# Two experts of different groups in one strip of slots: a mixture-of-experts stage with four experts at a time

## The chip, the cores and the metric

The kernel runs on one core of a Trainium2 chip, in one launch. The metric is the device time in microseconds. A core has five engines that run their own instruction streams side by side and meet only at semaphores: TensorE (PE; the loading of its stationary operand is shown apart, as PEld), VectorE (DVE), ScalarE (ACT), GpSimd (POOL) and SyncE (SP). In this kernel SP does little but issue the loads of weights, in one fixed order.

## The reference

A decoder trunk of two layers over 256 tokens of width 1024, in float32. In each layer four attention mixers are summed into the residual, and then a mixture of experts is added:

```
lc  = x2 @ w_coarse + b_coarse              # 4 groups
grp = argmax(lc);  p_grp = softmax(lc)[grp]  # one group for a token
lf  = (x2 @ w_fine + b_fine)[grp]           # its 8 experts
two best of the eight, softmax over the two, times p_grp
x  <- x + gate2 * sum_e weight_e * (silu(a_e) * b_e) @ w2[e],   a_e, b_e = split(x2 @ w13[e])
```

There are 32 experts (4 groups of 8), w13 of 1024 x 512 and w2 of 256 x 1024 for each; so a layer reads 32 x 3.1 MB = 100.7 MB of expert weights, whatever the tokens choose. Each token goes to two experts of one and the same group. The change concerns only this part.

## The kernel before, in words

**The expert stage** (`experts`, from line 2015). The router (`route`) gives each token a rank among the tokens of its expert (`rk`) and a weight (`W`, split into a high and a low part). An expert has a strip of 64 slots (`CAP`), and two experts share the 128 rows of the array. For each of 16 pairs p the loop from line 2109 does this:

- `selection` makes 0/1 matrices from tokens to slots by comparing ranks with a row of slot numbers; `selection_t` transposes them, and `slot_weights` brings the tokens' weights to the slots. These serve two pairs (four strips) at once.
- `gather_bank`, in four banks for two pairs: the normalised tokens, as a high and a low part (`hh`, `hl`), are multiplied by the selection into 256 columns, scaled and shifted by the layer's modulation on the way out.
- `first`: the slots of the pair times w13, eight steps of 128 rows; expert e fills half e of the 128 output rows. `swiglu` and `hidden_t` make the hidden rows and transpose them.
- `second`: the hidden rows times w2, in two halves of 512 columns; `weighted` multiplies by slot weight and gate and splits into high and low.
- `scatter`, one turn later: the transposed selection brings the slots back to the tokens, into four accumulators that hold the residual stream and stay open for the whole stage.

`more_rounds` would repeat all this for experts with more than 64 tokens; its loop runs only if there are any.

**The loads.** `plan_all` fixes the order of all weight loads, and `advance` issues the next ones, on SP, as soon as a buffer is free: a ring of 8 buffers of 1 MB, and pages of 512 KB. A half of w13 (1 MB) takes a ring buffer or two pages, a half of w2 (512 KB) takes a page. `done` gives a buffer back after its last matmul. The order of the loads is the order of use, so a load that waits for its buffer holds up all behind it. After the last expert's weights come the first ones of the next layer (`in`, `ada`).

The order on TensorE around the stage is that of the program text: in turn p the first projection, the scatter of pair p-1, gather banks of the next two pairs, the hidden transposes, then the second projection:

```
            g = first(p)                                            # line 2119
            ...
                scatter(acc, ST[(p - 1) // 2][:, (p - 1) % 2], ys, False)
            if nxt:
                prep_g(q + 1, 3 * i)
            gT = hidden_t(g)
            if nxt and i == 0:
                prep_g(q + 1, 1)
                prep_g(q + 1, 2)
            elif nxt:
                prep_t(q + 1)
            ys = second(p, gT)                                      # line 2133
```

In layer 0 the small weights of layer 1's router (`load_weights`) and compression are fetched by ScalarE in turn 4. Names in the profile: `pg` pages, `ring` ring buffers, `at` working accumulators, `mm` the open ones, `gt` intermediate rows, `K` constants (the identity among them), `W` token weights.

Of the kernel before, what the change touches and what calls it, by code (L numbers as in the profile page):

```python
# [22 lines left out]
CAP = 64  # L23
# [235 lines left out]
def kernel(ctx, tc, x_in, c_in, w_ada, b_ada, norm_gain, w_in, qk_gain, cmp_pe, cmp_w1, cmp_w2,  # L259
# [1555 lines left out]

    rk = cst.tile([128, 2, NE], FT, name="rk")

    W = cst.tile([128, 2, 2, NE], FR, name="W")
    NRt = cst.tile([1, 17], I32, name="NRt")
# [3 lines left out]
    all1 = one_b.to_broadcast([128, 128])  # L1823

    def route(l, rs, lo):
# [29 lines left out]

        oh = T_("smb", [128, 2, 32], BF)
        V.tensor_tensor(oh, o12[:, :, 0], o12[:, :, 1], op=OP.add)
        p, tot = at([128, 2, 32]), at([128, 32])
        T.matmul(p[:, 0], tri, oh[:, 0], start=True, stop=True)
# [12 lines left out]
        V.tensor_scalar(rk, rk, -1.0, None, op0=OP.add)  # L1872
        cm = sm(16)
        V.tensor_reduce(cm[0:1], tot[0:1].rearrange("p (a b) -> p a b", b=2), axis=AX.X, op=OP.max)

        def further():

            nr = sm(17)
            V.tensor_scalar(nr[0:1, 0:16], cm[0:1], float(CAP), None, op0=OP.is_gt)
            for m in (2, 3):  # L1880
                V.scalar_tensor_tensor(nr[0:1, 0:16], cm[0:1], float(m * CAP), nr[0:1, 0:16], op0=OP.is_gt, op1=OP.add)
            V.tensor_reduce(nr[0:1, 16:17], nr[0:1, 0:16], axis=AX.X, op=OP.max)
            V.tensor_copy(NRt, nr[0:1])

        def weights():
# [4 lines left out]
            V.tensor_scalar(w3[:, :, 0], w3[:, :, 0], 0.5, None, op0=OP.mult)  # L1890
            V.tensor_tensor(w3[:, :, 1], w3[:, :, 0], e2, op=OP.mult)
            V.tensor_tensor(o12, o12, w3[:, :, :, None].to_broadcast([128, 2, 2, 32]), op=OP.mult)
            V.tensor_tensor(o12[:, :, 0], o12[:, :, 0], o12[:, :, 1], op=OP.add)
            split(W[:, :, 0], W[:, :, 1], o12[:, :, 0])

# [20 lines left out]
    def slot_weights(sel, ws, n):  # L1916
        p = at([128, n // 2, 2, 2])
# [4 lines left out]
        w = sm(n // 2)  # L1922
        for e in range(2):
            V.tensor_reduce(w[64 * e:64 * e + 64], p[64 * e:64 * e + 64, :, :, e], axis=AX.X, op=OP.add)
        return w

# [18 lines left out]

    def swiglu(p):
        th = T_("gt", [128, 256])
        A.activation(th, p[:, 0:256], AF.Tanh, scale=0.5)
        g = T_("gt", [128, 256])
        V.scalar_tensor_tensor(g, th, 1.0, p[:, 0:256], op0=OP.add, op1=OP.mult)  # L1950
        V.tensor_tensor(g, g, p[:, 256:512], op=OP.mult)
        return g

    def hidden_t(g):
        p = at([128, 2, 128])
        for k in range(2):
            T.transpose(p[:, k], g[:, 128 * k:128 * k + 128], ID)
        t = T_("gt", [128, 2, 128])
        A.activation(t, p, AF.Copy)
# [15 lines left out]
    def more_rounds(l, acc):  # L1975
        tot = nc.values_load(NRt[0:1, 16:17], min_val=0, max_val=3)
        with tc.If(tot > 0):
            with tc.For_i(0, NE // 2) as pi:
                rks = T_("sm", [128, 2, 2])
                V.tensor_copy(rks, rk[:, :, ds(2 * pi, 2)])  # L1980
                wsl = T_("sm", [128, 2, 2, 2], FR)
                V.tensor_copy(wsl, W[:, :, :, ds(2 * pi, 2)])
                rounds = nc.values_load(NRt[0:1, ds(pi, 1)], min_val=0, max_val=3)
                with tc.For_i(0, rounds):
                    V.tensor_scalar(rks, rks, float(-CAP), None, op0=OP.add)
                    sel, st = selection(rks, 2)
                    selection_t(sel, st, 2)
                    w = slot_weights(sel, wsl, 2)
# [3 lines left out]
                    p = at([128, 512])  # L1992
                    for k in range(KT):
                        for e in range(2):
                            t = T_("gt", [128, 512])
                            G.dma_start(t, w13[l, ds(2 * pi + e, 1), 128 * k:128 * k + 128, :]
                                              .rearrange("a p n -> p (a n)"))
                            T.matmul(p[64 * e:64 * e + 64], xg[k // 4][:, k % 4, 64 * e:64 * e + 64], t, start=k == 0,
                                     stop=k == KT - 1)
                    gT = hidden_t(swiglu(p))  # L2000
                    for n in range(2):
                        p = at([128, 512])
                        for k in range(2):
                            for e in range(2):
                                t = T_("gt", [128, 512])
                                G.dma_start(t, w2[l, ds(2 * pi + e, 1), 128 * k:128 * k + 128,
                                                        512 * n:512 * n + 512].rearrange("a p n -> p (a n)"))
                                T.matmul(p[64 * e:64 * e + 64], gT[:, k, 64 * e:64 * e + 64], t, start=k == 0,
                                         stop=k == 1)
                        y = weighted(p, w, MOD[l, "g2"][:, 512 * n:512 * n + 512])  # L2010
# [4 lines left out]
    def experts(l):  # L2015
# [40 lines left out]

        NP = NE // 2
        SEL, ST, SW, XG = {}, {}, {}, {}

# [4 lines left out]
        def prep_t(q):  # L2064
            selection_t(SEL[q], ST[q], 4)
            SW[q] = slot_weights(SEL[q], W[:, :, :, 4 * q:4 * q + 4], 4)

        def prep_g(q, b, eng=None):
            gather_bank(l, SEL[q], 4, b, XG[q], eng or (V if b % 2 else A))

        def first(p):
            q, i = divmod(p, 2)
            h = at([128, 512])
            for k in range(KT):
                for e in range(2):
                    w = piece(("w13", l, 2 * p + e, k // 4), (k % 4) * 512, 512)
                    c = 128 * i + 64 * e
                    T.matmul(h[64 * e:64 * e + 64], XG[q][k // 4][:, k % 4, c:c + 64], w,
                             start=k == 0, stop=k == KT - 1)
                if k % 4 == 3:  # L2080
                    for e in range(2):
                        done(("w13", l, 2 * p + e, k // 4))
            return swiglu(h)

        def second(p, gT):
            ys = []
            for n in range(2):
                y = at([128, 512])
                for k in range(2):
                    for e in range(2):  # L2090
                        w = tiles[("w2", l, 2 * p + e, k)]
                        T.matmul(y[64 * e:64 * e + 64], gT[:, k, 64 * e:64 * e + 64], w[:, 512 * n:512 * n + 512],
                                 start=k == 0, stop=k == 1)
                ys.append(weighted(y, SW[p // 2][:, p % 2:p % 2 + 1], MOD[l, "g2"][:, 512 * n:512 * n + 512]))
            for k in range(2):
                for e in range(2):
                    done(("w2", l, 2 * p + e, k))
            return ys
# [10 lines left out]
        for p in range(NP):  # L2109
            q, i = divmod(p, 2)  # L2110
            nxt = q + 1 < NP // 2
            if nxt and i == 0:
                prep_sel(q + 1)
            if l + 1 < DEPTH and p == 4:
                load_weights(l + 1)
                load_cw2(l + 1)
            if l + 1 < DEPTH and p == NP - 1:
                tables()
            g = first(p)
            if p == 0:  # L2120
                filler(2 - FILL)
                prep_t(0)
            else:
                scatter(acc, ST[(p - 1) // 2][:, (p - 1) % 2], ys, False)
# [83 lines left out]
```

## Time and profile before

| | |
|---|---|
| median of 3 runs | 1080.46 us (1079.86 to 1084.5) |
| profiled execution | 1081.84 us, its span 1080.1 us |
| TensorE busy | 1038.0 us, 96% of the span |
| VectorE, ScalarE busy | 597.3 us (55%), 446.0 us (41%) |
| moved from memory | 335.36 MB, 311 GB/s over the span |
| expert stages, first to last projection | 311 to 548 us (layer 0), 834 to 1071 us (layer 1) |

A busy TensorE is not a TensorE at its peak, since matmuls are pipelined; for its pace one reads the starts of its matmuls in the timeline. An f32 matmul has two records in the trace, and those of the two halves of the array stand side by side. The rate of the loads is read by stage, not over the span.

### The profile page before, as it was taken

The page shows a single profiled execution, that of the slowest core. Times are in us where ns is not written, and L with a number is a line of the kernel's source. Part 1 is how long each engine was busy: PE and PEld are TensorE (multiplying, and loading weights), DVE is VectorE, ACT ScalarE, POOL GpSimd, SP SyncE. Part 2 cuts the span into 40 slices and gives each one's busy share as a digit, 9 for nine tenths or more (in the row PEclk, how much of TensorE's full clock was granted, in tenths as well). Part 3 has the DMA queues.
Part 4 walks back from the last instruction along what each step waited for, and adds up shares of the span by engine and source line. Part 5 has one row for each costly group of instructions (what it writes and reads, how often), then busy time and mean ns, then how long its engine had stood idle before and what let it go on. Part 6 is the DMA issues. An engine that isn't in the chain of part 4 may idle for free. (4 is left out here: it accounts for less than half of the span.)

```text
span 1080.1 us, 15489 instructions
## 1 busy us (share of the span) xinstructions
PE 1038.0 (96%) x5615; PEld 654.6 (61%) x5616; DVE 597.3 (55%) x1316; ACT 446.0 (41%) x1089; POOL 136.4 (13%) x273
## 2 busy tenths in 40 slices
PE   5989999999999999999999989999999999999997
PEld 2557777787854455544446867778876554555542
DVE  1657678988653332333356885986876233333332
ACT  1554857754441222222146467667444222221211
POOL 0021444320010000000001342530201000000000
PEclk8999999999999999999999999999999999999999
DMA  9977765678899999999967784557779799999991
GB/s 337 412 240 285 270 203 198 219 274 312 311 346 362 410 343 410 411 412 412 413 237 239 267 335 162 197 195 255 290 262 373 265 410 352 411 412 410 412 393 40
DMA packets 151057, 337.50 MB, mean 312 GB/s; under 512 B 13197, under 2 KB 30909, under 8 KB 150973
## 3 DMA queue, kind: packets, MB, share of 16 engines
q1 hardware_dynamic: 144166, 334.66, 82.4%
q10 hardware_dynamic: 6678, 1.77, 0.7%
q8 instruction: 46, 0.75, 0.3%
q14 instruction: 39, 0.31, 0.1%
q0 software_dynamic: 128, 0.02, 0.0%
HBM read 335.36 MB, written 1.05 MB: 311 GB/s over the span
## 5 line engine op out<-in xcount | busy, mean ns | idle before, releaser
L253 PE MATMUL mm<-pg 128*128 128x512 f32 (+4 forms) x1984 | 467.8, 387 | 9.4 <-DVE pg L253 6.0
L253 PEld LDWEIGHTS mm<-pg 128*128 128x128 f32 x1984 | 350.8, 188 | 122.6 <-issue 36.6
L253 PE MATMUL at<-ring,pg 128*64 128x512 f32 (+2 forms) x912 | 241.1, 560 | 2.4 <-POOL pg L253 2.4
L253 PE MATMUL at<-pg 128*128 128x256 f32 (+6 forms) x1192 | 226.6, 363 | 3.1 <-ACT pg L253 1.9
L253 DVE TENSOR_TENSOR pg<-ring,pg 128x512 fp32r<-128x512 f32 (+4 forms) x276 | 182.1, 696 | 65.1 <-ACT pg L253 63.2
L253 PEld LDWEIGHTS at<-pg 128*128 128x128 f32 (+3 forms) x1192 | 130.5, 167 | 71.1 <-issue 56.8
L253 ACT ACTIVATE pg<-ring 128x512 fp32r<-128x512 f32 (+4 forms) x276 | 148.5, 600 | 18.2 <-DMA wr<-in_w_fine_dram 5.0
L253 PEld LDWEIGHTS at<-ring,pg 128*64 128x64 f32 (+2 forms) x912 | 80.4, 135 | 100.4 <-issue 87.0
L253 PE MATMUL at<-pg,gt 128*64 128x512 f32 x512 | 116.9, 598 | 2.1 <-ACT gt L253 2.1
L253 ACT ACTIVATE gt<-at 128x256 f32<-128x256 f32 x64 | 24.6, 384 | 214.5 <-PE at L253 207.8
L253 DVE SCALAR_TENSOR_TENSOR gt<-gt,at 128x256 f32<-128x256 f32 x32 | 13.5, 421 | 148.4 <-ACT gt L253 148.4
L253 ACT ACTIVATE pg<-gt 128x512 fp32r<-128x512 f32 x64 | 40.3, 629 | 115.5 <-DVE gt L253 115.5
L253 DVE SCALAR_TENSOR_TENSOR gt<-at,sm,pg 128x512 f32<-128x512 f32 x64 | 47.9, 748 | 61.7 <-PE at L253 61.7
L253 ACT ACTIVATE pg<-pg,sm 128x128 f32<-128x128 f32 (+2 forms) x168 | 70.1, 458 | 16.1 <-DVE sm L253 11.4
L253 ACT ACTIVATE pg<-at 128x512 f32<-128x512 f32 (+5 forms) x106 | 50.0, 502 | 54.1 <-PE at L253 53.8
L253 PEld LDWEIGHTS at<-pg,gt 128*64 128x64 f32 x512 | 33.9, 136 | 60.0 <-issue 51.7
L253 DVE TENSOR_TENSOR pg<-gt,pg 128x512 fp32r<-128x512 f32 x64 | 44.3, 692 | 45.7 <-ACT pg L253 44.3
L253 DVE TENSOR_SCALAR pg<-at,A,mod 128x256 f32<-128x256 f32 x64 | 31.7, 539 | 60.1 <-PE at L253 60.1
L253 PE MATMUL at<-K,pg 128*128 128x128 f32 (+1 forms) x388 | 59.4, 282 | 4.1 <-DVE pg L253 2.3
L253 ACT ACTIVATE gt<-mm 128x512 f32<-128x512 f32 x44 | 25.8, 595 | 78.6 <-PE mm L253 77.3
L253 DVE SCALAR_TENSOR_TENSOR pg<-ring,cs,pg 128x1024 f32<-128x1024 f32 x44 | 58.1, 1320 | 0.1
L253 PEld LDWEIGHTS at<-K,pg 128*128 128x128 f32 (+1 forms) x388 | 46.3, 143 | 18.3 <-DVE pg L253 4.7
(162 smaller groups left out, 678.7 us busy)
## 6 DMA issues: line engine op xcount, KB each, us to landing
pg<-in_w_dram SPq DMA_DIRECT2D x196, 512.0 KB, 10.9
ring<-in_w_dram SPq DMA_DIRECT2D x94, 1024.0 KB, 11.9
ring<-in_w_ada_dram SPq DMA_DIRECT2D x45, 1024.0 KB, 8.0
ring<-in_w_in_dram SPq DMA_DIRECT2D x33, 1024.0 KB, 4.8
ring<-in_cmp_w_dram SPq DMA_DIRECT2D x8, 1024.0 KB, 6.5
ring<-in_w_branch_dram SPq DMA_DIRECT2D x8, 1024.0 KB, 4.9
ring<-in_w_out_dram SPq DMA_DIRECT2D x8, 1024.0 KB, 4.8
ring<-in_w_in_dram SPq DMA_DIRECT2D x8, 976.0 KB
```

Source lines behind the costliest of these rows:

```text
L253: return f(*args, **kw)
```

## The change

A strip of 64 slots now belongs to two experts of different groups: expert p + 8s and expert p + 16 + 8s (s is the strip, 0 or 1; the second term is `b`). Since a token's two experts are of one group, it stands in a strip at most once. A turn of the loop handles two strips and four experts, so there are 8 turns in a layer. Selection, gather, slot weights, weighting and scatter are done once for a strip. Both experts' first projections run over all 64 slots; a mask of the slots (`m`, a third row of `W`) keeps of each slot the half of its own expert: `first_half` copies the first expert's product times its mask, `swiglu` adds the second's times the other mask, and then writes the hidden rows twice, once under each mask. The second projection sums both experts into the same accumulator. The loads of a turn are 8 halves of w13 and then 8 halves of w2. The fetch of layer 1's small weights moves from turn 4 of 16 to turn 2 of 8.

```diff
+    def expert(p, b, s):
+        return p + 16 * b + 8 * s
...
-            for p in range(NE // 2):
-                for hf in range(2):
-                    for e in range(2):
-                        add(("w13", l, 2 * p + e, hf))
-                for k in range(2):
-                    for e in range(2):
-                        add(("w2", l, 2 * p + e, k))
+            for p in range(NE // 4):
+                for b in range(2):
+                    for hf in range(2):
+                        for s in range(2):
+                            add(("w13", l, expert(p, b, s), hf))
+                for b in range(2):
+                    for k in range(2):
+                        for s in range(2):
+                            add(("w2", l, expert(p, b, s), k))
...
-        V.tensor_tensor(oh, o12[:, :, 0], o12[:, :, 1], op=OP.add)
+        o4 = o12.rearrange("p t i (h s u) -> p t u s (i h)", h=2, s=2)
+        for t in range(2):
+            V.tensor_reduce(oh[:, t].rearrange("p (u s) -> p u s", s=2), o4[:, t], axis=AX.X, op=OP.max)
...
+    def first_half(p, m):
+        t = T_("gt", [128, 512])
+        A.activation(t, p, AF.Copy, scale=m)
+        return t
+
-    def swiglu(p):
+    def swiglu(p, t, m):
+        V.scalar_tensor_tensor(t, p, m[1], t, op0=OP.mult, op1=OP.add)
         th = T_("gt", [128, 256])
-        A.activation(th, p[:, 0:256], AF.Tanh, scale=0.5)
-        g = T_("gt", [128, 256])
-        V.scalar_tensor_tensor(g, th, 1.0, p[:, 0:256], op0=OP.add, op1=OP.mult)
-        V.tensor_tensor(g, g, p[:, 256:512], op=OP.mult)
+        A.activation(th, t[:, 0:256], AF.Tanh, scale=0.5)
+        V.scalar_tensor_tensor(th, th, 1.0, t[:, 0:256], op0=OP.add, op1=OP.mult)
+        g = T_("gt", [128, 2, 256])
+        for b in range(2):
+            V.scalar_tensor_tensor(g[:, b], th, m[b], t[:, 256:512], op0=OP.mult, op1=OP.mult)
...
         def second(p, gT):
-            ys = []
-            for n in range(2):
-                y = at([128, 512])
+            ys = [at([128, 512]) for _ in range(2)]
+            for b in range(2):
+                for n in range(2):
+                    for k in range(2):
+                        for e in range(2):
+                            w = tiles[("w2", l, expert(p, b, e), k)]
+                            T.matmul(ys[n][64 * e:64 * e + 64], gT[:, b, k, 64 * e:64 * e + 64],
+                                     w[:, 512 * n:512 * n + 512], start=b == 0 and k == 0, stop=b == 1 and k == 1)
+                    if b:
+                        ys[n] = weighted(ys[n], SW[p // 2][:, p % 2:p % 2 + 1], MOD[l, "g2"][:, 512 * n:512 * n + 512])
                 for k in range(2):
                     for e in range(2):
-                        ...
+                        done(("w2", l, expert(p, b, e), k))
...
-            g = first(p)
+            h = first(p, 0)
...
+            h = first_half(h, masks(p)[0])
+            g = swiglu(first(p, 1), h, masks(p))
```

On TensorE, in the steady part of layer 0's expert stage, a turn of the program before, with two experts, from the scatter to the beginning of the next first projection (`mm<-pg` scatter, `at<-pg 128x256` gather, `at<-K,gt` hidden transposes, `at<-pg,gt` second projection, `at<-ring,pg` first projection):

```order
L253 MATMUL mm<-pg 128x512 x8
L253 MATMUL at<-pg 128x256 x8
L253 MATMUL at<-K,gt 128x128 x2
L253 MATMUL at<-pg 128x256 x16
L253 MATMUL at<-pg,gt 64x512 x8
L253 MATMUL at<-ring,pg 64x512 x8
```

And the same place in the changed program, a turn with four experts (here the other kind of turn, with the slot transposes `at<-K,pg` and slot weights `at<-W,pg`):

```order
L253 MATMUL mm<-pg 128x512 x8
L253 MATMUL at<-pg 128x256 x8
L253 MATMUL at<-K,gt 128x128 x4
L253 MATMUL at<-K,pg 128x128 x4
L253 MATMUL at<-W,pg 128x6 x4
L253 MATMUL at<-pg,gt 64x512 x16
L253 MATMUL at<-ring,pg 64x512 x17
```

Scatter and gather stand there with the same counts for four experts as before for two; hidden transposes and projections have twice the count.

On SP, in the same stage, the loads of one turn before (four halves of w13, `128x4x512` in the ring or twice `128x2x512` in pages, then four halves of w2, `128x1024`), with the semaphores that each waits for (DMAHW0 to 7 are those of earlier loads, PE and DVE stand for a buffer's last user):

```order
L320 DMA ring<-in_w_dram 128x4x512 [waits DMAHW0_49]
L320 DMA ring<-in_w_dram 128x4x512 [waits DMAHW1_49]
L320 DMA pg<-in_w_dram 128x2x512 [waits DMAHW2_49,PE_49]
L320 DMA pg<-in_w_dram 128x2x512 [waits DMAHW3_49,PE_49]
L320 DMA ring<-in_w_dram 128x4x512 [waits DMAHW4_49,PE_49]
L320 DMA pg<-in_w_dram 128x1024 [waits DMAHW5_49]
L320 DMA pg<-in_w_dram 128x1024 [waits DMAHW6_49]
L320 DMA pg<-in_w_dram 128x1024 [waits DMAHW7_49,PE_49]
L320 DMA pg<-in_w_dram 128x1024 [waits DMAHW0_49,DVE_49,PE_49]
```

And in the changed program, the last two halves of w13 of a turn, and its eight halves of w2:

```order
L320 DMA ring<-in_w_dram 128x4x512 [waits DMAHW0_49,PE_49]
L320 DMA ring<-in_w_dram 128x4x512 [waits DMAHW1_49,PE_49]
L320 DMA pg<-in_w_dram 128x1024 [waits DMAHW2_49]
L320 DMA pg<-in_w_dram 128x1024 [waits DMAHW3_49]
L320 DMA pg<-in_w_dram 128x1024 [waits DMAHW4_49]
L320 DMA pg<-in_w_dram 128x1024 [waits DMAHW5_49]
L320 DMA pg<-in_w_dram 128x1024 [waits DMAHW6_49,PE_49]
L320 DMA pg<-in_w_dram 128x1024 [waits DMAHW7_49,DVE_49,PE_49]
L320 DMA pg<-in_w_dram 128x1024 [waits DMAHW0_49,DMASW0_49,PE_49]
L320 DMA pg<-in_w_dram 128x1024 [waits DMAHW1_49,DVE_49]
```

Eight loads of w2 now follow each other, of which the last four wait for a page that an engine still uses.

## Rows read from the trace of the kernel before

**Rows 1.** Windows: start:end, length, busy time by engine, clock, DMA share, GB/s.

```profile
311.20:387.20 76.00, 75.79 (x398) 37.79 (x400) 25.24 (x52) 18.48 (x37) 0.00 (x0) 1.00 0.96 359
387.20:529.70 142.50, 142.50 (x736) 69.91 (x733) 48.44 (x94) 29.93 (x59) 0.00 (x0) 1.00 1.04 408
...
834.30:918.30 84.00, 84.00 (x434) 41.08 (x435) 28.05 (x57) 19.41 (x39) 0.00 (x0) 1.00 0.91 345
...
1050.00:1053.00 3.00, 3.00 (x15) 1.64 (x12) 0.84 (x2) 0.38 (x1) 0.00 (x0) 1.00 0.65 265
```

**Rows 2.** The page: rate of the loads in 40 equal slices of the span.

```profile
GB/s 337 412 240 285 270 203 198 219 274 312 311 346 362 410 343 410 411 412 412 413 237 239 267 335 162 197 195 255 290 262 373 265 410 352 411 412 410 412 393 40
```

**Rows 3.** Timeline of TensorE, four experts in layer 0: start, length, operation, count.

```profile
438.62 2.11 PE L253 MATMUL mm<-pg 128*128 128x512 f32 x8
...
441.65 2.16 PE L253 MATMUL at<-pg 128*128 128x256 f32 x16
443.74 3.65 PE L253 MATMUL at<-pg,gt 128*64 128x512 f32 x16
447.22 3.60 PE L253 MATMUL at<-ring,pg 128*64 128x512 f32 x16
...
454.19 2.14 PE L253 MATMUL mm<-pg 128*128 128x512 f32 x8
456.16 1.10 PE L253 MATMUL at<-pg 128*128 128x256 f32 x8
457.10 0.38 PE L253 MATMUL at<-K,gt 128*128 128x128 f32 x2
457.32 0.60 PE L253 MATMUL at<-K,pg 128*128 128x128 f32 x4
...
458.19 3.65 PE L253 MATMUL at<-pg,gt 128*64 128x512 f32 x16
...
468.64 0.73 PE L253 MATMUL mm<-pg 128*128 128x512 f32 x2
```

**Rows 4.** Waits, 387 to 530 us: total us, times, longest (weight loads; SP's queue).

```profile
PEld at L253 <- DMA pg<-in_w_dram: 0.6, 2, 0.3
SPq L320 <- PE at L253: 32.6, 24, 4.0
```

**Rows 5.** Timeline of SP: the last issues of expert weights, layer 0, layer 1.

```profile
514.96 4.80 SPq L320 DMA_DIRECT2D pg<-in_w_dram  x4
...
1037.28 4.81 SPq L320 DMA_DIRECT2D pg<-in_w_dram  x4
```

**Rows 6.** Timeline of TensorE, the ends of the two expert stages.

```profile
544.87 3.65 PE L253 MATMUL at<-pg,gt 128*64 128x512 f32 x16 [0.53 <-ACT gt L253]
...
559.37 1.06 PE L253 MATMUL mm<-ring,cs 128*32 128x512 f32 x8
...
1064.68 2.11 PE L253 MATMUL mm<-pg 128*128 128x512 f32 x8
...
1067.55 3.65 PE L253 MATMUL at<-pg,gt 128*64 128x512 f32 x16 [0.53 <-ACT gt L253]
```

**Rows 7.** Groups by shape, 403 to 530 us: busy us, mean ns, idle before.

```profile
L253 DVE SCALAR_TENSOR_TENSOR gt<-at,sm,pg 128x512 f32<-128x512 f32 x16 | 12.0, 748 | 13.7 <-PE at L253 13.7
...
L253 ACT ACTIVATE gt<-at 128x256 f32<-128x256 f32 x17 | 6.5, 384 | 57.2 <-PE at L253 57.2
L253 DVE SCALAR_TENSOR_TENSOR gt<-gt,at 128x256 f32<-128x256 f32 x9 | 3.8, 422 | 40.2 <-ACT gt L253 40.2
...
L253 ACT ACTIVATE pg<-at 128x512 fp32r<-128x512 f32 x4 | 2.4, 597 | 0.0
```

**Rows 8.** Start of the program: timeline of TensorE; a window as in rows 1.

```profile
13.04 1.06 PE L253 MATMUL mm<-ring,cs 128*32 128x512 f32 x8 [0.72 <-DMA ring<-in_w_ada_dram]
...
18.18 1.93 PE L253 MATMUL mm<-ring,cs 128*32 128x512 f32 x8 [4.08 <-DMA ring<-in_w_ada_dram]
...
16.00:27.00 11.00, 8.46 (x38) 6.27 (x39) 3.32 (x11) 3.53 (x8) 0.00 (x0) 0.55 1.03 406
```

More of the change, by code (lines that the diff above doesn't have):

```diff
@@ L1823, with strips_of @@
     all1 = one_b.to_broadcast([128, 128])
+    def strips_of(v):
+        return v.rearrange("p t (h s u) -> p t h u s", h=2, s=2)
     def route(l, rs, lo):
@@ L1891, in weights @@
             V.tensor_tensor(w3[:, :, 1], w3[:, :, 0], e2, op=OP.mult)
+            for t in range(2):
+                V.tensor_tensor(W[:, t, 2].rearrange("p (u s) -> p u s", s=2), *[
+                    o12[:, t, i, 0:16].rearrange("p (s u) -> p u s", s=2) for i in range(2)], op=OP.add)
             V.tensor_tensor(o12, o12, w3[:, :, :, None].to_broadcast([128, 2, 2, 32]), op=OP.mult)
-            V.tensor_tensor(o12[:, :, 0], o12[:, :, 0], o12[:, :, 1], op=OP.add)
-            split(W[:, :, 0], W[:, :, 1], o12[:, :, 0])
+            ws = T_("smb", [128, 2, 16])
+            for t in range(2):
+                V.tensor_reduce(ws[:, t].rearrange("p (u s) -> p u s", s=2), o4[:, t], axis=AX.X, op=OP.add)
+            split(W[:, :, 0], W[:, :, 1], ws)
         return further, weights
@@ L1921, in slot_weights @@
                          ws[:, t, :, 2 * i:2 * i + 2], start=t == 0, stop=t == 1)
-        w = sm(n // 2)
+        w, m = sm(n // 2), sm(n)
+        m = m.rearrange("p (b i) -> p b i", b=2)
         for e in range(2):
-            V.tensor_reduce(w[64 * e:64 * e + 64], p[64 * e:64 * e + 64, :, :, e], axis=AX.X, op=OP.add)
-        return w
+            r = slice(64 * e, 64 * e + 64)
+            V.tensor_reduce(w[r], p[r, :, 0:2, e], axis=AX.X, op=OP.add)
+            V.tensor_copy(m[r, 0], p[r, :, 2, e])
+        V.tensor_scalar(m[:, 1], m[:, 0], -1.0, 1.0, op0=OP.mult, op1=OP.add)
+        return w, m
     def gather_bank(l, sel, n, q, xg, eng):
@@ L1991, in more_rounds @@
                         gather_bank(l, sel, 2, q, xg, V)
[L1992 to L1999, printed above, removed]
@@ L2000, in more_rounds @@
-                    gT = hidden_t(swiglu(p))
+                    ms, t1 = [m[:, b] for b in range(2)], None
+                    for b in range(2):
+                        p = at([128, 512])
+                        for k in range(KT):
+                            for e in range(2):
+                                t = T_("gt", [128, 512])
+                                G.dma_start(t, w13[l, ds(pi + (16 * b + 8 * e), 1), 128 * k:128 * k + 128, :]
+                                                  .rearrange("a p n -> p (a n)"))
+                                T.matmul(p[64 * e:64 * e + 64], xg[k // 4][:, k % 4, 64 * e:64 * e + 64], t, start=k == 0,
+                                         stop=k == KT - 1)
+                        if b == 0:
+                            t1 = first_half(p, ms[0])
@@ L2001, in more_rounds @@
+                    gT = hidden_t(swiglu(p, t1, ms))
                     for n in range(2):
                         p = at([128, 512])
[L2003 to L2009, printed above, removed]
+                        for b in range(2):
+                            for k in range(2):
+                                for e in range(2):
+                                    t = T_("gt", [128, 512])
+                                    G.dma_start(t, w2[l, ds(pi + (16 * b + 8 * e), 1), 128 * k:128 * k + 128,
+                                                      512 * n:512 * n + 512].rearrange("a p n -> p (a n)"))
+                                    T.matmul(p[64 * e:64 * e + 64], gT[:, b, k, 64 * e:64 * e + 64], t,
+                                             start=b == 0 and k == 0, stop=b == 1 and k == 1)
@@ L2055, in experts @@
         seeds(1)
[L2057 to L2058 removed]
+        NP = NE // 4
+        SEL, ST, SW, SM, XG = {}, {}, {}, {}, {}
         def prep_sel(q):
@@ L2065, in prep_t, with first @@
             selection_t(SEL[q], ST[q], 4)
-            SW[q] = slot_weights(SEL[q], W[:, :, :, 4 * q:4 * q + 4], 4)
+            SW[q], SM[q] = slot_weights(SEL[q], W[:, :, :, 4 * q:4 * q + 4], 4)
         def prep_g(q, b, eng=None):
             gather_bank(l, SEL[q], 4, b, XG[q], eng or (V if b % 2 else A))
-        def first(p):
+        def first(p, b):
             q, i = divmod(p, 2)
@@ L2075, in first @@
                 for e in range(2):
-                    w = piece(("w13", l, 2 * p + e, k // 4), (k % 4) * 512, 512)
+                    key = "w13", l, expert(p, b, e), k // 4
                     c = 128 * i + 64 * e
-                    T.matmul(h[64 * e:64 * e + 64], XG[q][k // 4][:, k % 4, c:c + 64], w,
+                    T.matmul(h[64 * e:64 * e + 64], XG[q][k // 4][:, k % 4, c:c + 64], piece(key, (k % 4) * 512, 512),
                              start=k == 0, stop=k == KT - 1)
@@ L2081, in first, with masks @@
                     for e in range(2):
-                        done(("w13", l, 2 * p + e, k // 4))
-            return swiglu(h)
+                        done(("w13", l, expert(p, b, e), k // 4))
+            return h
+        def masks(p):
+            return [SM[p // 2][:, b, p % 2:p % 2 + 1] for b in range(2)]
         def second(p, gT):
-            ys = []
-            for n in range(2):
-                y = at([128, 512])
+            ys = [at([128, 512]) for _ in range(2)]
+            for b in range(2):
+                for n in range(2):
+                    for k in range(2):
+                        for e in range(2):
+                            w = tiles[("w2", l, expert(p, b, e), k)]
[3 more added lines that the diff above has]
+                        ys[n] = weighted(ys[n], SW[p // 2][:, p % 2:p % 2 + 1], MOD[l, "g2"][:, 512 * n:512 * n + 512])
                 for k in range(2):
                     for e in range(2):
[L2091 to L2097, printed above, removed]
+                        done(("w2", l, expert(p, b, e), k))
             return ys
@@ L2113, in experts @@
                 prep_sel(q + 1)
-            if l + 1 < DEPTH and p == 4:
+            if l + 1 < DEPTH and p == 2:
                 load_weights(l + 1)
@@ L2122, in experts @@
                 prep_t(0)
-            else:
+            h = first_half(h, masks(p)[0])
+            g = swiglu(first(p, 1), h, masks(p))
+            if p:
                 scatter(acc, ST[(p - 1) // 2][:, (p - 1) % 2], ys, False)
```

37 lines of the change are left out of this document (18 added, 19 removed).

## The prediction

> **What bounds the kernel now.** I began with the windows of the expert stages [rows 1]: TensorE is busy for all 142.5 of 142.5 us, which would suggest that any work taken from it shortens the program. The page's line of load rates warns against that [rows 2]: in slices 16 to 20 and 33 to 38, the later part of the two layers' expert stages, the loads run at 410 to 413 GB/s (one at 352), and no slice of the whole program shows more than 413. So two things are near their limit at once, and the question is which is ahead of the other, and by how much.
>
> The timeline of TensorE gives its pace [rows 3]. Two turns of the loop handle four experts: from the scatter at 438.62 to the scatter at 468.64, 30.02 us. The pace of the loads is 408 GB/s from 387 to 530 us [rows 1] and 411 at its steadiest [rows 2]. Four experts have eight loads of 1.05 MB and eight of 0.52 MB, 12.58 MB, which is 30.6 us at 411 GB/s. The loads are thus the slower of the two already, by 0.6 us in 30, and TensorE doesn't feel it because it lives on a stock: in the second half of layer 0 the weight loads into the array wait 0.6 us in all for an expert's load [rows 4]. At the end of a layer the stock can be read off. The last expert load of layer 1 is in the last issue group, 1037.28 plus 4.81, so issued by 1042.1 [rows 5]; the window from 1050 to 1053 moves at 265 instead of 411 GB/s [rows 1], so the stream ends at 1050 + 3 x 265/411 = 1051.9. The last second projection, which uses that load, starts only at 1067.55 [rows 6]. In layer 0 the last group is issued by 514.96 + 4.80 = 519.8 [rows 5]; with the lag of layer 1 (9.8 us) it lands at 529.6, and its projection starts at 544.87 [rows 6]. The stock at the end is 15.6 us in layer 1 and 15.3 us in layer 0.
>
> **The change part by part.** *What TensorE loses.* For four experts there is one scatter instead of two (454.19 to 456.16: 1.97 us), two gather banks instead of four (441.65 to 443.74: 2.09 us), and half of the slot transposes and slot weights (457.32 to 458.19: 0.87, half is 0.44) [rows 3]. First and second projections and the transposes of the hidden rows keep their count. 30.02 - 4.50 = 25.5 us, 36.0 us in a layer of eight such steps, 72 us in the program, if nothing else limited it.
>
> *What the loads allow.* No byte is saved: 12.58 MB for four experts, as before. Once TensorE has used up its stock of 15 us it waits, so most of the 36 us cannot be had. The end of a layer is then counted from the landing of its last load. The last eight loads are now the second-projection weights, 4.19 MB or 10.2 us of the stream; so the last first-projection load lands 10.2 us before the end of it. Behind that one come half of a first projection (a whole one takes 6.97, 447.22 to 454.19 [rows 3]: 3.5), and the way from the end of it to the second projection, 2.87 (1064.68 to 1067.55 [rows 6]) plus what the way gains: on VectorE a product over 512 columns at 0.75 and one more over 256 at 0.42 [rows 7], and four transposes and a 512-wide copy where two and 256 stood, some 0.3; 4.3 together. The second projection starts 10.2 - 7.8 = 2.4 us before the stream ends, runs twice 3.48 us, and ends 4.6 us after it. Before, it ended 15.6 + 3.5 = 19.1 us after it in layer 1 and 18.8 us in layer 0. That gives 14.5 and 14.2 us. It is the stock, given back; this is the firm part of the sum, 28.7 us.
>
> *What the stream itself gains.* It was held up by full buffers early in each expert stage: 359 GB/s over 76 us in layer 0, 345 over 84 us in layer 1 [rows 1]. Against 411 that is 9.6 and 13.5 us, the most that earlier freed buffers can return. They come free 4.5 us earlier at each step, the first ones not at all earlier, and in layer 0 the router and compression weights for layer 1 still go out in the middle of the stage. The other end is nothing. I take 5 us in each layer, near the middle and nearer the low end in layer 1, where the first window is the emptiest.
>
> *What is added, and its cover.* Masking the first expert's half is one ScalarE copy of 128x512 (597 ns), and the merge one VectorE operation like the 748 ns one [rows 7]; both engines are busy for less than half of the time here (48 and 30 of 142.5 us [rows 1]), and weighting and splits, halved in count, pay for it. The merge waits for the second of the two first projections; behind it on VectorE stand that step's gather evacuation, weighting and splits, all of which come later on TensorE too, so nobody waits for them sooner. In a full step the scatter and a gather bank (454.19 to 457.10: 2.91 [rows 3]) stand between the last first-projection matmul and the hidden transposes and cover the chain of 0.75 + 0.38 + three times 0.42 = 2.39 [rows 7], with its hand-overs just so; where that cover is gone, in the last two steps of a layer, the 1.2 us more is in the 4.3 above. The router is changed by a few operations on 16 instead of 32 columns, some more reduces of about 0.2 us, on a path of some 10 us: between -0.5 and +1 us in each layer; I take 0.
>
> *What the next layer meets.* Its first loads follow on the same stream: two of 1.05 MB and four of 1.05 MB land 5.1 and 15.3 us after the last expert load. TensorE used the four at 559.37 [rows 6], 11.0 us after the end of the last second projection at 548.35; now that is 4.6 + 11.0 = 15.6 us after the stream's end. They are just in time; layer 0's gain survives, with a microsecond or two at risk.
>
> *The sum.* The profiled execution took 1081.84 us, its span 1080.1; the median of the three runs is 1080.46. 14.2 + 14.5 + 5 + 5 = 38.7: a profiled time of 1043, and 1041.8 for the median. With the two unknown stream terms at their upper ends it is 28.7 + 23.1 = 51.8, or 1028.7; at nothing, 1051.8.
>
> The Trainium skill, DMA: Bandwidth & Descriptors, Specifications, gives 435 GB/s as the fabric's ceiling and about 358 GB/s as a core's share of HBM. The trace decides against the second: 411 GB/s stood for over 120 us. By the first, as an estimate, the long stretches of some 140 us would end 8 us earlier each, and the time would be about 1025; no slice of the page shows a rate above 413, so it stays out of the sum.
>
> **The rivals.**
> *TensorE sets the pace after all.* Then all 72 us but the longer chains are saved, about 1014 us. For it: TensorE has no idle time in 142.5 us [rows 1]. Against it: 100.7 MB in eight steps of 25.5 us would need 493 GB/s. 3%.
>
> *The loads set it already, nothing is gained.* 1080 us. For it: 30.6 against 30.0 us. Against it: were it so, the last load would be used when it lands, not 15 us later. It could still come true if a stage needed that stock for an irregularity that I don't see. 5%.
>
> *The eight pages stop the stream (slower).* A step's eight second-projection weights go only into pages, where four did before, and the last ones wait for pages that TensorE frees in the second projection of a step before; the first-projection loads of the next step stand behind them on the same queue. Already now the queue waits for TensorE 24 times, 4.0 us at the longest, 32.6 us in 142 [rows 4], hidden since up to eight loads are under way (the eight semaphores that its issues wait for in turn). If every one of the 16 steps lost a stretch t of the stream, the time is 1041.8 + 16 t: no gain at t = 2.4, slower by 0.5% from 2.8 us, 1106 at 4.0. Against it: a page is freed by the first half of the second projection now, and eight loads under way are 10 to 20 us of the stream. 5%.
>
> *The clock falls while TensorE waits (slower).* The start of the program shows it: after 4.08 us of waiting for a load eight matmuls took 1.93 us, where the same eight had taken 1.06, and the granted clock of 16 to 27 us was 0.55, mostly the lower level, 1.2 GHz [rows 8]. In the last two steps of each layer TensorE will wait some 1.7 us before a pair of first-projection loads (5.1 us of stream for 3.5 us of matmuls). If that dropped the clock for those four steps, each would take some 19 us longer: 1118 us. Against it: after a wait of 0.72 us the eight took the 1.06 us, and 1.7 lies nearer to that than to 4.08. 3%. The Trainium skill, TensorE: Matmul & The Clock Gate, HAM oscillation, warns of just this, a kernel whose short blocks of matmuls alternate with waits for loads and which starts each block cold; the row of 18.18 agrees with it, the wait here is shorter.
>
> That the change doesn't do what it says would be a strip of more than 64 tokens, which sends the program through the rounds loop; the reference's router, worked out on its own inputs, puts 52 and 53 tokens at most on a strip in the two layers. 1%.
>
> **How the numbers follow.** My forecast, the stream sets the end, has 83% and the range 1028 to 1056 by its two bounds and the risk at the next layer's start. The rivals have 3, 5, 5, 3 and 1%. For 8 in 10 I take 1028 to 1058. A measurement of this kernel can tell about 0.5% from no change, 5.4 us: faster has the forecast and the first rival and a little of the third, 87%; the same 5%; slower 8%.
>
> **What would show it.** Right: in both layers' last two steps first projections of 18 to 20 us, with TensorE idle for the expert loads; loads at 411 GB/s until a few microseconds before the layer's last projection; the steps before at about 25.5 us; the last second projection ending 4 to 6 us after the last load. Wrong: a step of 25.5 us up to the end (the first rival), loads below 400 GB/s in the second half of a stage with the queue waiting for TensorE (the pages), or a granted clock below 1 there.

## The result, and the profile after

The changed kernel takes 1065.91 us (median of 4 runs, 1063.65 to 1068.41) against 1080.64 (1079.86 to 1084.5) for the kernel before: a ratio of 0.986 [0.982, 0.989] (in brackets, here and below, the 95% interval). The sign was forecast, the size was not: 14.7 us are gained where 38.7 were forecast, and 1065.9 lies above the range of 1028 to 1058. The profiled execution took 1063.65 us, its span 1062.0.

In the page of the changed kernel, the line of load rates, 40 slices of the span, to be held against [rows 2]:

```profile
GB/s 354 398 261 268 282 205 199 191 286 336 300 339 375 394 346 392 395 394 395 394 394 277 259 327 162 201 193 244 288 339 242 350 364 394 395 395 395 391 391 207
```

No slice reaches 400. Where the kernel before stood at 410 to 413 for many slices, this one stands at 391 to 395. The second slice matters most: 398 instead of 412 [rows 2], although the two programs do the same there. Windows of the kernel before, from 27 to 54 us (columns as in [rows 1]: window, length, PE, PEld, DVE, ACT, POOL, clock, DMA share, GB/s):

```profile
27.00:54.00 27.00, 26.11 (x135) 16.08 (x133) 18.38 (x48) 15.03 (x35) 1.94 (x2) 1.00 1.03 411
```

The same window of the changed kernel, and three stretches of its expert stages (early part and later part of layer 0, later part of layer 1):

```profile
27.00:54.00 27.00, 25.67 (x132) 15.38 (x131) 17.80 (x47) 14.20 (x33) 1.94 (x2) 1.00 1.04 397
...
311.30:387.30 76.00, 74.65 (x377) 32.72 (x379) 18.45 (x43) 13.96 (x26) 0.00 (x0) 1.00 1.02 368
387.30:531.30 144.00, 128.35 (x580) 49.71 (x576) 29.21 (x58) 17.12 (x30) 0.00 (x0) 1.00 1.04 394
...
909.00:1045.00 136.00, 122.60 (x542) 47.93 (x538) 26.40 (x54) 15.87 (x28) 0.00 (x0) 0.99 1.04 395
```

So the loads are slower at 27 us already, long before an expert's weight is read, and they are slower while the DMA engines are busy all the time (share 1.04). In the later part TensorE is now busy for 128 of 144 us, where it was busy without a gap [rows 1]; the clock stays up.

What TensorE waits for is seen in the timeline of the end of layer 1 (start, length, operation, count, idle time before and what ended it), which answers to [rows 6]:

```profile
1011.70 2.11 PE L253 MATMUL mm<-pg 128*128 128x512 f32 x8
...
1035.66 1.07 PE L253 MATMUL at<-ring,pg 128*64 128x512 f32 x2 [0.39 <-DMA ring<-in_w_dram]
1038.37 3.65 PE L253 MATMUL at<-ring,pg 128*64 128x512 f32 x14 [1.63 <-DMA ring<-in_w_dram]
1041.94 2.11 PE L253 MATMUL mm<-pg 128*128 128x512 f32 x8
...
1045.88 7.09 PE L253 MATMUL at<-pg,gt 128*64 128x512 f32 x32 [0.69 <-ACT gt L253]
```

From scatter to scatter the last step takes 30.24 us, where 25.5 was worked out for TensorE's own pace, and the first projections in it wait for loads of w13 in the ring. And the waits from 387 to 530 us, which answer to [rows 4] (total us, times, longest):

```profile
PEld at L253 <- DMA ring<-in_w_dram: 23.8, 12, 2.8
...
SPq L320 <- PE at L253: 28.3, 17, 3.6
SPq L320 <- DMA ring<-in_w_dram: 22.0, 10, 2.6
```

The weight loads into the array wait 23.8 us for expert loads, where it was 0.6. SP's queue waits for TensorE no more than before (28.3 against 32.6), so the eight pages of the third rival do not hold the stream. What it waits for more than before are loads that are still under way: 22.0 us for those into the ring, where it was 9.6.

What differs at 27 us? Not the instructions, but the addresses. All buffers for loads follow the small tables in each partition of on-chip memory. The change made three of those shorter: `rk` from 256 to 128 bytes, `W` from 512 to 384, `NRt` from 68 to 36, 288 bytes together with its rounding. In the built programs the ring begins at byte 26880 of a partition before, which is 105 x 256, and at 26592 after, a multiple of 32 and not of 64; the buffers are multiples of 4096 long, so every one of them is shifted alike. The records of the loads' packets (a packet is one unbroken run of a load) show a difference of that kind: before, 97% of the 88,832 packets of 2048 bytes took 84 ns; after, 43% did, and most of the others 85 to 96.

### The profile page after: what moved, and what is told of

It reads as the page before. It is cut to its first block, busy times and chain, and to the rows that moved or that the text cites. A ratio compares the mean times of both kernels' runs of the same rounds, so it can differ in the third digit from the quotient of the medians.

```text
span 1062.0 us, 14314 instructions
## 1 busy us (share of the span) xinstructions
PE 991.4 (93%) x5167; PEld 598.9 (56%) x5168; DVE 538.2 (51%) x1220; ACT 407.5 (38%) x1001; POOL 136.5 (13%) x273
## 5 line engine op out<-in xcount | busy, mean ns | idle before, releaser
L253 PE MATMUL mm<-pg 128*128 128x512 f32 (+4 forms) x1856 | 435.0, 387 | 11.6 <-DVE pg L253 5.3
L253 PEld LDWEIGHTS mm<-pg 128*128 128x128 f32 x1856 | 330.3, 189 | 106.1 <-issue 22.8
L253 PE MATMUL at<-ring,pg 128*64 128x512 f32 (+3 forms) x888 | 241.9, 566 | 26.1 <-DMA ring<-in_w_dram 24.5
L253 PE MATMUL at<-pg 128*64 128x512 f32 (+6 forms) x960 | 193.8, 390 | 5.3 <-ACT pg L253 2.5
L253 PEld LDWEIGHTS at<-pg 128*64 128x64 f32 (+3 forms) x960 | 96.5, 160 | 62.6 <-issue 42.2
L253 DVE SCALAR_TENSOR_TENSOR gt<-at,sm,gt 128x512 f32<-128x512 f32 x16 | 12.0, 751 | 214.6 <-PE at L253 214.6
L253 DVE SCALAR_TENSOR_TENSOR gt<-at,sm,pg 128x512 f32<-128x512 f32 x32 | 23.9, 748 | 86.3 <-PE at L253 75.6
L253 ACT ACTIVATE pg<-gt 128x512 fp32r<-128x512 f32 x32 | 20.1, 630 | 114.0 <-DVE gt L253 114.0
L253 PEld LDWEIGHTS at<-K,pg 128*128 128x128 f32 (+1 forms) x356 | 43.7, 146 | 17.7 <-issue 4.4
L253 ACT ACTIVATE gt<-at,sm 128x512 f32<-128x512 f32 x16 | 11.0, 688 | 97.4 <-PE at L253 79.6
L253 POOL TENSOR_TENSOR pg<-pg,gt 128x512 f32<-128x512 f32 x16 | 29.6, 1874 | 107.3 <-DVE gt L253 107.3
## 6 DMA issues: line engine op xcount, KB each, us to landing
ring<-in_w_dram SPq DMA_DIRECT2D x91, 1024.0 KB, 13.1
```

Of the source, the lines that this page charges most:

```text
L253: return f(*args, **kw)
```

## The experiments

Theory A is that the address does it; B, that the order of the loads does (eight of w2 in a row); C, that the rate differs from run to run whatever the program.

**The addresses, within the kernels (e1 to e4, on one chip).** e1 is the changed kernel again; the others have one line more:

```diff
     sb = ctx.enter_context(tc.tile_pool(name="sb", bufs=1))
+    sb.tile([128, 8], FT, name="pad", tag="pad", bufs=1)     # e2, and e4 on the kernel before; 24 in e3
```

> The changed kernel as it is, a second time. Theory A (addresses): since the change made a few small tables shorter, all load buffers begin at 26592 bytes in a partition instead of 26880, which is a multiple of 32 but not of 64 bytes, and that slows every load; expected: saturated slices at 392 to 395 GB/s again, the same stretch at the start (27 to 54 us) at 397, 1064 to 1068 us. Theory B (the order of the loads and the eight w2 loads in a row slow the stream): the same numbers in the expert stages, but no reason for 397 at the start. Theory C (the rate of memory differs from run to run): anything between 392 and 412 GB/s, time between 1042 and 1068.

> The changed kernel with an unused 32 bytes ahead of the buffers, so that they begin at 26624, a multiple of 512; nothing else differs. A: 410 to 412 GB/s in the saturated slices and 411 at 27 to 54 us, and the time falls by about 20 us against e1, to 1042 to 1048. B: 392 to 395 GB/s in the expert stages and e1's time. C: the rate and the time of e1, since both run on one chip, or a difference without order.

> As e2 with 96 bytes: the buffers begin at 26688, a multiple of 64 but not of 128 or 256. If a multiple of 64 is what counts, e2's rate and time (410 GB/s, 1042 to 1048 us); if a multiple of 256 is, e1's (394 GB/s, 1066) or something between. B and C: e1's numbers.

> The kernel before with 32 unused bytes ahead of its buffers, so that they begin at 26912, not a multiple of 64. A: 392 to 397 GB/s where it had 410 to 412, the saturated steps of the loads then 31.9 us against TensorE's 30.0, so the stock of 15 us shrinks by about 10 us in each layer and hides nearly all of it: 1080 to 1086 us. B and C: 411 GB/s, 1080 us.

| run | start of the ring | median us | ratio to before |
|---|---|---|---|
| before | 26880 = 105 x 256 | 1080.45 | |
| e1, changed | 26592, 224 past a multiple of 256 | 1064.9 | 0.985 [0.983, 0.988] |
| e2, changed + 32 bytes | 26624 = 104 x 256 | 1045.83 | 0.969 [0.965, 0.973] |
| e3, changed + 96 bytes | 26688, 64 past | 1063.33 | 0.983 [0.981, 0.986] |
| e4, before + 32 bytes | 26912, 32 past | 1081.05 | 1.000 [0.999, 1.002] |

Thirty-two unused bytes are worth 19 us. The load rates on the page of e2:

```profile
GB/s 356 412 235 278 276 209 232 162 280 300 345 316 383 388 364 412 412 411 413 411 409 287 247 322 172 199 193 228 281 362 217 346 383 411 412 412 412 410 410 211
```

The rate is back at 410 to 413 with the changed kernel's order of loads, in a run beside e1 on one chip: B and C fall. One part of A's expectation did not come as it was put: from 27 to 54 us e2 shows 398 GB/s, not 411. The loads pause at the end of that stretch (share 0.81 from 50 to 54 us); up to 50 us they run at 410. Windows of e2, the last three in its expert stages:

```profile
27.00:54.00 27.00, 25.72 (x131) 15.41 (x130) 18.00 (x46) 14.50 (x33) 1.94 (x2) 1.00 1.00 398
27.00:50.00 23.00, 22.34 (x119) 13.20 (x117) 14.59 (x40) 12.99 (x30) 0.84 (x2) 1.00 1.03 410
50.00:54.00 4.00, 3.37 (x13) 2.21 (x13) 3.41 (x7) 1.51 (x3) 1.09 (x1) 1.00 0.81 331
311.70:387.70 76.00, 74.69 (x378) 32.76 (x380) 18.40 (x43) 13.90 (x26) 0.00 (x0) 1.00 1.01 378
387.00:530.00 143.00, 132.41 (x610) 52.24 (x608) 29.67 (x59) 17.71 (x31) 0.00 (x0) 1.00 1.04 411
816.30:900.30 84.00, 82.69 (x414) 35.42 (x416) 21.23 (x47) 15.20 (x28) 0.00 (x0) 1.00 1.00 383
```

And the stretch up to 50 us of the kernel before, then of the changed kernel:

```profile
27.00:50.00 23.00, 22.34 (x120) 13.35 (x119) 14.38 (x40) 12.43 (x30) 0.00 (x0) 1.00 1.03 411
```

```profile
27.00:50.00 23.00, 22.34 (x119) 13.11 (x117) 14.40 (x40) 12.69 (x30) 0.92 (x2) 1.00 1.04 396
```

The windows of e3 and of e4 from 387 to 530 us:

```profile
387.00:530.00 143.00, 129.29 (x578) 49.89 (x574) 28.50 (x57) 17.12 (x30) 0.00 (x0) 0.99 1.04 394
```

```profile
387.00:530.00 143.00, 142.47 (x738) 70.19 (x732) 47.51 (x93) 30.29 (x60) 0.00 (x0) 1.00 1.04 392
```

A multiple of 64 isn't enough (e3). And the kernel before loses the same rate when it is shifted (e4), but no time that can be measured: the last expert loads land at 534.5 and 1058.7 us instead of 529.7 and 1052.6, and its stock covers that (some 10 us of it were expected to go in each layer, 4.8 and 6.1 went). So the times of the kernel before could not show the price of an address.

**The loads alone (e5).** 32 loads of 1 MB for each start:

```diff
+    for kind, N in (("w13", 32), ("w2", 32)):                 # runs of 2048, then of 4096 bytes
+        for o in OFF:                                         # 0, 32, 64, 96, 128, 160, 192, 256, 0 bytes
+            for i in range(N):                                #   past a multiple of 512
+                t = sb.tile([128, 2048 + 128], FT, name="ring", tag="ring", bufs=8)
+                v = t[:, o // 4:o // 4 + 2048]
...
+                    nc.sync.dma_start(v.rearrange("p (k n) -> p k n", n=512), src)
```

> Loads alone, no computing (it leaves out the whole computation): 32 loads of 1 MB for each of nine starts in the buffers, 0, 32, 64, 96, 128, 160, 192, 256 and again 0 bytes past a multiple of 512, eight loads under way as in the kernel; first with runs of 2048 bytes (w13), then with runs of 4096 (w2). Theory A with a multiple of 256 as the rule: 410 to 413 GB/s at 0, 256 and 0, and 392 to 397 at all others, 128 included. With a multiple of 128 as the rule: 128 is fast too. Rival: the start matters only beside a working TensorE (contention for the buffers' memory), then all nine stretches are alike, at 410 to 425 GB/s. If each packet costs a fixed extra, runs of 4096 lose half the share of runs of 2048.

Windows inside the stretches of 0, 32, 64, 128 and 256 bytes with runs of 2048, then 0, 32 and 128 with runs of 4096 (columns: window, length, POOL, clock, DMA share, GB/s):

```profile
30.00:80.00 50.00, 0.00 (x0) 1.00 1.05 409
110.00:165.00 55.00, 0.00 (x0) 1.00 1.04 387
196.00:250.00 54.00, 0.00 (x0) 1.00 1.04 387
370.00:425.00 55.00, 0.00 (x0) 1.00 1.05 387
630.00:680.00 50.00, 0.00 (x0) 1.00 1.05 409
795.00:845.00 50.00, 0.00 (x0) 1.00 1.02 421
875.00:925.00 50.00, 0.00 (x0) 1.00 1.02 410
1120.00:1170.00 50.00, 0.00 (x0) 1.00 1.03 410
```

A start off a multiple of 256 costs 5.4% with runs of 2048 bytes and 2.6% with runs of 4096, and it makes no difference by how much it is off: all six such starts gave 387, and 409 or 410. TensorE isn't needed for it. From the packets' records, the mean of a packet of 2048 goes from 84.0 to 88.1 to 88.8 ns and that of 4096 from 159.0 to 163.4 to 163.8: some 4.5 ns a packet in the mean, whatever its length. The 387 lies below the 392 to 397 that was expected from the kernels, where a third of a stage's bytes has runs of 4096: e5's rates weighted so give 394, and 413 from a multiple of 256, and the kernels show 394 and 411. The Trainium skill, DMA: Bandwidth & Descriptors, How a descriptor splits into AXI transactions, gives a rule with this boundary, told for reads: pieces of 256 bytes that must start at a multiple of 256, and an extra piece for a start that doesn't. The boundary agrees with e5, for the address that is written to; that the extra grows with the bytes below the start, as its table has it, e5 does not show.

**Does the stream set the end (e6)?**

```diff
-                for b in range(2):     # loads of w13, and of w2
+                for b in range(1):
...
-                    key = "w13", l, expert(p, b, e), k // 4
+                    key = "w13", l, expert(p, 0, e), k // 4     # and the same for w2
```

> The changed kernel with buffers from 26624 (as e2), and the loads of the second expert of each strip left out: its products use the first one's weights, so half of the expert weights isn't read. TensorE's work is the same. If the stream sets the end, as forecast, TensorE's own pace of 25 us per four experts holds to the end of both stages, and the time falls from e2's 1045.8 by about 20 us in each layer, to 1000 to 1014. If something else than the stream held e2's last steps (hand-overs, pages), it stays at 1040 or more.

1020.56 us, a ratio of 0.942 [0.939, 0.945], on a chip where the kernel before takes 1083.05. The stages keep TensorE's pace, seen in TensorE's timeline at the end of layer 0 (the scatter ahead of the last second projection, and that projection):

```profile
506.20 2.11 PE L253 MATMUL mm<-pg 128*128 128x512 f32 x8
510.15 7.09 PE L253 MATMUL at<-pg,gt 128*64 128x512 f32 x32 [0.69 <-ACT gt L253]
```

That second projection starts at 524.07 in e2 and at 531.98 in the changed kernel, while all three begin their first projection between 311 and 313. The line of e2, then of the changed kernel:

```profile
524.07 7.09 PE L253 MATMUL at<-pg,gt 128*64 128x512 f32 x32 [0.69 <-ACT gt L253]
```

```profile
531.98 7.09 PE L253 MATMUL at<-pg,gt 128*64 128x512 f32 x32 [0.69 <-ACT gt L253]
```

So with the start mended too the loads hold the end of the stage, by some 14 us where 20 were expected; the time came out 6 us above the expectation. Half the loads also need fewer pages, but e2's loads run at 411 GB/s from 387 to 530 us (its window above), so it is their rate that holds them there, not a wait for pages.

**Toward a better kernel (e7 to e12).** e7 and e11 are e2 again, on another chip. e8 moves a fetch:

```diff
             if l + 1 < DEPTH and p == 2:
-                load_weights(l + 1)
                 load_cw2(l + 1)
...
             R_.append(c)
+            if l and len(R_) == 150:      # some way into layer 1's mixers
+                load_weights(l)
```

> e2 a second time, as the neighbour that e8 is to be compared with: 1043 to 1050 us, the saturated slices at 410 to 413 GB/s.

> e2 with the fetch of layer 1's router weights (two loads of many short rows, on ScalarE's queue) moved out of layer 0's expert stage into layer 1's mixers. In e2 SP waits 10.1 us in that stage for these two. If that is what the stream of layer 0 loses, the time falls by 3 to 8 us against e7, to 1038 to 1043; if SP would have waited for full buffers then anyway, it stays within 1.5 us of e7.

e7 took 1050.05 us, 0.969 [0.966, 0.972], e8 1047.82, 0.967 [0.965, 0.969]. The two waits of SP are gone in e8; in e2 they were, from 311 to 420 us:

```profile
SPq L321 <- DMA wr<-in_w_fine_dram: 5.2, 1, 5.2
SPq L321 <- DMA wr<-in_w_coarse_dram: 4.9, 1, 4.9
```

Of these 10.1 us about 2 may come back: between first projection and last expert load of layer 0 e8 needs 212.3 us, e2 214.6. By the times alone it stays inconclusive, since the intervals overlap; SP would mostly have waited for full buffers anyway.

e9 uses the 421 GB/s of e5: w13 in runs of 4096 bytes.

```diff
-            two(key, 512, w13, ((l * NE + e) * D + hf * 512) * 512, 512)
+            two(key, 1024, w13, ((l * NE + e) * D + hf * 512) * 512, 1024)
...
-                    T.matmul(p[:, i], src[t][:, 128 * kt:128 * kt + 128], ...
+                    T.matmul(p[:, i], src[t][:, 256 * q + i:256 * q + 256:2], ...
...
+        pairs_of_rows(l)          # scale and shift in the new order: 16 small matmuls, one copy on VectorE
         further, weights = route(l, rs, lo)
```

> The changed kernel with buffers from 26880 (a multiple of 256), and w13 read in runs of 4096 bytes: partition p takes rows 2p and 2p+1 of each 256 instead of rows p and 128+p, and the gather takes every second column to match. e5 moved runs of 2048 bytes at 409 GB/s and runs of 4096 at 421. w13 is 67.1 MB of a layer's 100.7; if the stream sets the end, that is 4.7 us in each layer: the time falls from e2's 1045.8 (ratio 0.9686 to the kernel before) by 7 to 10 us, to 1036 to 1039 (ratio 0.959 to 0.962), with 418 to 421 GB/s in the saturated slices. If something else held e2's end, it stays at 0.967 to 0.970; if the reads of every second column slow the gather, TensorE's steps grow beyond 25 us early in a stage.

> e9 and e8 together: the longer runs, and the router weights of layer 1 fetched in its mixers. If e8's fetch really cost the stream of layer 0 some 2 us (e8 stood at 0.967 [0.965, 0.969] beside e7's 0.969 [0.966, 0.972], which does not tell), 2 us below e9; otherwise e9's time.

> e2 a third time, as the neighbour that e9 and e10 are to be compared with: ratio 0.966 to 0.971, the saturated slices at 410 to 413 GB/s.

e9 took 1051.65 us, 0.971 [0.969, 0.974]; e10 1048.4, 0.969 [0.967, 0.971]; e11 1047.55, 0.968 [0.965, 0.970]. By the times alone e10's 3 us below e9 stay as inconclusive as e8's 2 below e7. The rate came as expected, 417 GB/s from 387 to 530 us and 419 to 420 in the saturated slices, and the time did not. The timeline of VectorE in e9 has the reason:

```profile
303.78 0.17 DVE L253 COPY p<-at 128x16 f32<-128x16 f32 x1 [5.19 <-PE at L253]
303.87 0.42 DVE L253 SCALAR_TENSOR_TENSOR smb<-at,sm,rbias 128x40 f32<-128x40 f32 x2
```

My copy stood ahead of the router on VectorE and waited 5.2 us for matmuls that TensorE did late; the router, the gather and the stage began by so much later, in both layers. e12 moves it:

```diff
+        pairs_of_rows(l)          # now ahead of the stage's other work, its copy on ScalarE
         filler(1)
         mm = router_part(l, 3)
```

> e10 with the sixteen small matmuls that reorder scale and shift moved to the stage's beginning, and their copy from VectorE to ScalarE. In e9 and e10 that copy stood on VectorE ahead of the router and waited 5.2 us for TensorE, and the first projection began at 317.8 in e9, not at 311.7 as in e2. If that is what ate the gain of the longer runs, both stages begin some 5 us earlier than in e10 and the time falls by 8 to 11 us, to a ratio of 0.958 to 0.962 (some 1038 us). If the stage only waits longer for its loads, with no gain from the earlier start, it stays at 0.967 to 0.971.

1038.57 us (1037.63 to 1040.21), 0.959 [0.958, 0.961]: the fastest of those that compute everything, where the changed kernel as it was stands at 0.986. The first projections begin at 309.4 and 811.2 us (e10: 316.5 and 820.5). e12 holds e8's change as well as e9's: from the first projection to the end of the last second projection its profile is 7.1 us shorter than e11's in layer 0, where both count, and 3.9 in layer 1, where only the longer runs do (4.7 expected). Its load rates:

```profile
GB/s 354 412 261 289 277 213 208 164 297 306 347 311 371 394 418 420 419 419 420 419 405 258 275 317 126 197 192 227 284 360 216 348 373 419 420 420 420 419 420 209
```

## Why the prediction was wrong

The step that failed is "what the stream itself gains": it was priced at 5 us in each layer, between nothing and 9.6 or 13.5, on the ground that no byte is saved and that the loads run at 411 GB/s as before. The rate itself was taken over from the kernel before. It fell to 394, by 4%, and since the stream sets the end, that is paid: to the landing of the last expert load the changed kernel needs 8 us more than e2 in each layer, twice the 4 that earlier freed buffers gave back. In numbers of the profiles (the last expert load's landing from the packets' records, good to about 1 us: by its very last packet the first of them, 529.7, is 530.7; us, layer 0 and layer 1):

| term | before | forecast gain | changed kernel | e2 |
|---|---|---|---|---|
| first projection to landing of the last expert load | 218.4, 218.4 | 5, 5 | 222.7, 222.4: -4.3, -4.0 | 214.6, 214.2: 3.8, 4.2 |
| that landing to the end of the last second projection | 18.7, 18.4 | 14.2, 14.5 | 4.9, 5.3: 13.8, 13.1 | 4.8, 5.2: 13.9, 13.2 |
| sum of gains | | 38.7 | 18.6 | 35.1 |

The sums agree with the profiled executions: 1081.84 - 1063.65 = 18.2 and 1081.84 - 1046.37 = 35.5. Point by point:

- *TensorE loses 4.5 us per four experts.* Right. The first steps take 25.0 and 26.1 us by turns (second projection to second projection), 25.5 in the mean, as worked out.
- *The stock is given back.* Right in both kernels, 26.9 and 27.1 us of 28.7; the last second projection ends 4.8 to 5.3 us after the landing, where 4.6 was forecast.
- *The loads allow no more.* Right; e6 shows it.
- *The stream gains 5 and 5 us.* Wrong in sign as the change was made, nearly right (3.8 and 4.2) where only the address is mended. There the mechanism shows: early in the stages e2's loads run at 378 and 383 GB/s (its windows above), where 359 and 345 stood [rows 1]. That the size came so near is in part luck, for the 5 was picked between two bounds and not worked out. My lower bound of nothing left out what lowers the rate; I weighed the order of the loads and the buffers, not where they lie.
- *The next layer meets its loads in time.* Right in e2, where layer 1's first projection starts 17.9 us earlier (816.3 against 834.3) after a gain of 17.7 in layer 0. In the changed kernel 9.5 are gained and 9.2 arrive.
- *Signs to look for.* First projections of the last two steps, said to be 18 to 20 us, take 19.4 to 19.7 in e2 and 19.4 to 22.4 in the changed kernel; but in e2 TensorE waits for loads in the last three steps already, not in two. Loads below 400 GB/s were named as a sign of the rival of the eight pages; the sign came, but without its other half, a longer wait for TensorE. The address was no rival of mine, and the clue could be had: the changed program's addresses differ from those of before by 288 bytes.
- *The other rivals.* The clock stays at 0.99 to 1.00 in the stages. TensorE's own pace would give some 1018 (e6's ratio of 0.942 on 1080.5), not 1014.

The forecast of 1042 lies 4 to 8 us below the three measurements of e2 (1045.83, 1047.55, 1050.05). Some 3.6 us of that are the terms above, 35.1 for 38.7.

## What to carry to other kernels

When a change alters the size of anything that is allocated ahead of buffers for loads, look at where the buffers begin: a start at a multiple of 256 bytes was worth 4% of the load rate here, and a pad of 32 bytes 19 us. A rate that the kernel before shows is a property of its addresses and of the length of its runs too; a kernel with a stock of early loads hides it, and a change that uses up the stock makes it the bound. And what is added to mend the stream must not stand ahead of the stage's first result on the same engine: one copy on VectorE waited 5.2 us, which ate the gain of the longer runs until it was moved (e9, e12).

## What the runs showed of the hardware

- The rate of loads into on-chip memory depends on the start address in a partition modulo 256 bytes: 409 against 387 GB/s with runs of 2048 bytes, 421 against 410 with runs of 4096, the same for starts 32, 64, 96, 128, 160 and 192 past; 256 past a multiple of 512 is as good as 0.
- Runs of 4096 bytes are 3% faster than runs of 2048 at the same 1 MB a load (421 and 409 GB/s), and a whole stage kept 419 to 420 with them while TensorE worked (e12).
- Two small loads of many short rows on ScalarE's queue stand in e2's profile as 10.1 us of waits of SP's queue, which loads into other buffers, and they are gone when those loads are moved (e8).
- Reading every second column of the gather's stationary operand cost next to nothing: a gather bank took 0.95 to 0.96 us in e9 and 0.94 to 0.95 in e2.
